# Diagonal blocks of a chunked triangular solve: 32x32 blocks inverted on VectorE, replaced by two 16x16 blocks per operation and a merge on TensorE

## The chip, the cores and the metric

The kernel runs on one NeuronCore of a Trainium2 chip. Its time is the device time of one execution in microseconds (us); the time of before is the median of three runs. Lower is better.

## The reference, cut to what matters

One layer of a hybrid backbone: a context of 256 tokens and 512 latent tokens pass through one input projection, then half of the channels through gated DeltaNet (8 heads of 128) and half through RWKV-7 (16 heads of 64), each in both directions, then through one output projection. Both mixers are computed in chunks of 64 tokens, and each chunk needs the inverse of a unit triangular 64x64 matrix. The DeltaNet one is written out in the reference:

```
lmat = jnp.where(strict, jnp.einsum('bhncd,bhnsd->bhncs', kb, k) * decay, 0.0)
eye = jnp.eye(CHUNK, dtype=jnp.float32)
tmat = lax.linalg.triangular_solve(eye + lmat, jnp.broadcast_to(eye, lmat.shape),
                                   left_side=True, lower=True, unit_diagonal=True)
u = tmat @ (v * beta[..., None])
wk = tmat @ (kb * jnp.exp(g)[..., None])
...
def step(state, inp):
    u_i, wk_i, attn_i, q_i, k_i, gl_i = inp
    v_new = u_i - wk_i @ state
    o_i = q_i @ state + attn_i @ v_new
    state = state * jnp.exp(gl_i)[..., None, None] + jnp.einsum('bhcd,bhce->bhde', k_i, v_new)
    return state, o_i
```

RWKV-7 is a scan over tokens in the reference; the kernel brings it to the same chunked form, so that one unit of work has three triangular systems (one DeltaNet head, two RWKV heads) for each chunk and direction.

## The kernel before, in words

The work is cut into 16 units, called mixers here and numbered 0 to 15: 0 to 7 are the eight head groups on the context (4 chunks each), 8 to 15 the same groups on the latents (8 chunks each). A mixer records these stages, each a method of class `Mix`:

- `prep_g`, `prep_r`, `prep_d`, `blocks` make, with TensorE transposes and products and DVE and ACT operations, the tile `Z` that holds all triangular matrices of the mixer. The transposes and products write PSUM tiles of the ring `pm` (two buffers, `br` in the rows), scratch goes to SBUF tiles of the ring `t` (four or five buffers).
- `send` writes the 32x32 diagonal blocks of `Z` to DRAM (`DA`), eight DMAs.
- `solve` reads them back with one block per partition (48 or 96 partitions, tile `solNL`), inverts them on DVE by 30 steps of elimination, two operations each (`solT`, then `solNL`), and writes them to DRAM (`DD`).
- `levels` loads them back and joins two 32x32 inverses into one of 64x64 by two bundles of 32x32 products on TensorE (`wm<-lt,Z`, then `pss<-Z,lt`).
- `chain` is the recurrence, 4 or 8 serial steps of small products, evacuations and state updates; one step on the latents begins with the ACT operation `Xs<-pss`.
- `outp` (latents only) norms, transposes and gates the result.

Around the mixers run the input projections (products of 128x128x512 or 128x128x256 on split fp32r halves: `hhi`, `hlo`, `chi`, `clo`, and `yh`, `yl` for the last four of 16 input tiles), the gate columns, and from latent group 3 (mixer 11) on the output projection, in four passes, whose products have `yh`, `yl` too. Latent groups 0 to 2 (mixers 8 to 10) use one lane of buffers, one after the other; from mixer 11 on two lanes alternate.

Nothing is ordered by hand. Class `Rec` records every operation and `Rec.schedule` plans the order of each engine when the program is built, by the operations' place in the recording, their dependencies and free buffers. Three rules of it matter here. When TensorE has nothing ready and has done little lately, the planner puts in a filler product on zeros (`wm<-zero`); projections marked as fills may be put anywhere that TensorE is free. A bundle is issued as a whole. And the buffers of a ring are given out in the order in which the recording created the tiles, not in the order in which they are ready:

```
                    e = t.pool.tags[t.key]
                    fs = [s for s in e[1] if s.free is not None]
                    if e[3] != t.order or not fs:
                        parked.setdefault((t.pool, t.key), []).append(o)
                        return
```

A mixer's stages are recorded whole before the next mixer's. All operations go through helpers, so every row of the profile has one line number, L705, and is told apart by its tiles.

Of the kernel before, what the change touches and what calls it, by code (L numbers as in the profile page):

```python
# [15 lines left out]
P = 128  # L16
DM = 2048
KT = DM // P
SEQ = 512
# [8 lines left out]

CST = {}
_off = 0  # L30
for _n, _w in (("ident", 128), ("bd", 128), ("mk0", 64), ("mk1", 64), ("sold", 4),
               ("mz0", 192), ("mz1", 192), ("scan", 512), ("ones", 128), ("cum0", 128), ("cum1", 128), ("hp0", 128), ("hp1", 128),
               ("sel", 2)):
    CST[_n] = (_off, _w)
    _off += _w
NCST = _off
NCST_KEEP, NCST_M = CST["mz0"][0], CST["ones"][0]
# [12 lines left out]
def constants():  # L50
    c = np.zeros((P, NCST), np.float32)

    def put(n, a):
        o, w = CST[n]
        c[:, o:o + w] = a

    i = np.arange(P)
    r, col = i[:, None], i[None, :]
    same = (r // 64) == (col // 64)
    s, t = r % 64, np.arange(64)[None, :]  # L60
    put("ident", np.eye(P))
    put("bd", same)
    put("mz0", np.concatenate([t > s, t >= s, t > s], 1))
    put("mz1", np.concatenate([t < s, t <= s, t < s], 1))
    put("mk0", np.where(t >= s, 0.0, -1e4))
    put("mk1", np.where(t <= s, 0.0, -1e4))
    put("scan", (np.arange(512)[None, :] % 64 != 0))
    put("ones", 1.0)
    row = np.arange(P)
    for ph, nj in ((0, 2), (1, 4)):  # L70
        d = (row // (3 * nj)) % 2
        c[:, CST["sold"][0] + 2 * ph] = -1.0 * (d == 0)
        c[:, CST["sold"][0] + 2 * ph + 1] = -1.0 * (d == 1)
    put("cum0", same & (r <= col))
# [11 lines left out]
def layout(inp):  # L86
# [22 lines left out]
    def put(n, a):  # L109
# [610 lines left out]
def bc(ap, shape):  # L720
    return ap.to_broadcast(list(shape))


class Mix:
# [250 lines left out]

    def send(self):
        k, i, ph, nj, S = self.k, self.i, self.ph, self.nj, self.k.S
        DA, DD = self.DD = [k.dp.tile([w, 4, 2, 3 * nj, 32, 32], F32, tag=f"{t}{ph}", bufs=2, name=k.nm(t))
                            for t, w in (("DA", 1), ("DD", 2))]
        DA = DA[0]  # L980
        for b in range(4):
            for d in range(2):
                S.dma_start(DA[b, d].rearrange("u s t -> s u t"), self.zdiag(b, d))

    def solve(self):
        k, i, ph, nb = self.k, self.i, self.ph, self.nb
        V, G, S = k.V, k.G, k.S
        (DA, DD), DA = self.DD, self.DD[0][0]
        N, L, tmp = k.solNL[:, 0], k.solNL[:, 1], k.solT
        m0 = k.cs("sold")[0:nb, 2 * ph:2 * ph + 1]  # L990
        m1 = k.cs("sold")[0:nb, 2 * ph + 1:2 * ph + 2]
        S.dma_start(L[0:nb], DA.rearrange("b d u s t -> (b d u) s t"))
        V.tensor_scalar_mul(N[0:nb], L[0:nb], m1)
        k.stt(N[0:nb], L[0:nb].rearrange("p s t -> p t s"), m0, N[0:nb], ALU.mult, ALU.add)
        G.memset(N[0:nb].rearrange("p s t -> p (s t)")[:, 0:1024:33], 1.0)
        for s in range(1, 31):
            r = 31 - s
            tv = tmp[0:nb, 0:r * s].rearrange("p (a b) -> p a b", b=s)
            shp = [nb, r, s]
            k.tt(tv, bc(N[0:nb, s + 1:32, s:s + 1], shp), bc(N[0:nb, s:s + 1, 0:s], shp), ALU.mult)  # L1000
            k.tt(N[0:nb, s + 1:32, 0:s], N[0:nb, s + 1:32, 0:s], tv, ALU.add)
        V.tensor_copy(L[0:nb], N[0:nb].rearrange("p s t -> p t s"))
        S.dma_start(DD.rearrange("w b d u s t -> (b d u) w s t"), k.solNL[0:nb])

    def levels(self):
        k, i, ph, nj, Z = self.k, self.i, self.ph, self.nj, self.Z
        V, S = k.V, k.S
        DN, DL = self.DD[1][0], self.DD[1][1]
        RT = self.t2("lt")[:, 0:96 * nj].rearrange("p (u t) -> p u t", t=32)
        for b in range(4):  # L1010
            bb = b % 2
            S.dma_start(RT[32 * b:32 * b + 32], (DN, DL)[bb][b, bb].rearrange("u s t -> s u t"))
            for d in range(2):
                S.dma_start(self.zdiag(b, d), (DL, DN)[d][b, d].rearrange("u s t -> s u t"))
        FC = (slice(32, 64), slice(0, 32))
        px = k.pmt("lx", "g")[:, 0:96 * nj].rearrange("p (u t) -> p u t", t=32)
        with k.rec.bundle():
            for j in range(nj):
                for e in range(3):
                    for b in range(4):  # L1020
                        d, q = b % 2, b // 2
                        rr, oo = slice(32 * b, 32 * b + 32), slice(32 * (b ^ 1), 32 * (b ^ 1) + 32)
                        k.mm(px[oo, e * nj + j], Z[rr, d, 2 * q + e, j, self.acol(q, FC[d])], RT[rr, e * nj + j])
        xs = self.t2("lt")[:, 0:96 * nj].rearrange("p (u t) -> p u t", t=32)
# [216 lines left out]
class Kernel:  # L1241
# [118 lines left out]
    def front(self):  # L1360
        S, V, A, G = self.S, self.V, self.A, self.G
# [10 lines left out]
        fc = {n: fp.tile([P, CST[n][1]], F32, name="f" + n) for n in ("ones", "sel")}  # L1372
# [47 lines left out]
        for kt in range(KT):  # L1420
            self.rec.shift = -self.cfg.get("fsh", 200)
            ps = self.pmt("ada", "g")[:, 0:256]
            for jj in range(2):
                j = 2 * kt + jj
                w = wa.pop(j)
                with self.rec.bundle():
                    for k in range(8):
                        g = k % 4
# [13 lines left out]
            t = fp.tile([P, 768], F32, tag="tmp", bufs=2, name=self.nm("ht"))  # L1442
# [12 lines left out]
            for k in range(4):  # L1455
                m = 128 if k == 3 else 96
# [9 lines left out]
        fp.release()  # L1466
        fq.release()
        lp = self.lp = self.pool("lp")
        self.solNL = lp.tile([96, 2, 32, 32], F32, name="solNL")
        self.solT = lp.tile([96, 256], F32, name="solT")  # L1470
# [9 lines left out]
        V.tensor_copy(self.cstm, fc[:, 0:NCST_M - NCST_KEEP])  # L1480

        def fcs(n):
            o, w = CST[n]
            return fc[:, o - NCST_KEEP:o - NCST_KEEP + w]

        e = self.cfg.get("eshift", 150)
        for k in range(4):
            mu, om = self.pc("mul", k)[0:96], self.dvo["oml"][0:96, k:k + 1]
            for ph in (1, 0):
# [3 lines left out]
                n, o = (512, 64) if ph else (256, 1)  # L1493
# [245 lines left out]

    def main(self):  # L1740
        self.u = {}
        self.tbufs = {"t": (4, 5), "lt": (1, 1), "ot": (0, 2), "dg": (1, 1)}
        self.mp = self.pool("mpA")
        defer = self.cfg.get("defer", [])
        for i in range(NSLOT):
# [199 lines left out]
```

## Time and profile before

| | |
|---|---|
| three runs | 2064.42, 2066.45, 2070.24 us; median 2066.45 us |
| profiled execution | 2065.16 us, of which the profile's span is 2063.4 us |
| TensorE (PE) busy | 1932.1 us, 94% |
| VectorE (DVE) busy | 1451.6 us, 70% |
| ScalarE (ACT), GpSimd (POOL) busy | 811.6 us, 575.9 us |
| mean granted TensorE clock | 0.977 |

A busy share is the time in which at least one instruction of the engine was under way. Matmuls overlap, and filler products count as busy, so that TensorE's real work is what is left after taking the fillers off. An fp32 product appears as two matmul records in the trace (pieces, below); one fp32r product is one.

### The profile page before, as it was taken

To read this page: it belongs to the slowest core of one execution; us is meant where nothing else is said; L and a number is where in the kernel's file an instruction comes from. 1 tells how busy PE (TensorE), PEld (TensorE's weight loads), DVE (VectorE), ACT (ScalarE), POOL (GpSimd) and SP (SyncE) were. 2 spreads that over 40 slices of the span, in tenths; PEclk is the share of its full clock that TensorE was granted. 3 is DMA by queue.
4 is the path that set the end of the run, shared out by engine and by line. 5 is a ranking of instruction groups with operands and counts; after the bars stand their busy time and mean duration, and the time that the engine had idled before them with its cause. 6 is when DMAs were issued, how large, how long until landed. Compare 5 with 4: busy or idle time off the path is not lost.

```text
span 2063.4 us, 43525 instructions
## 1 busy us (share of the span) xinstructions
PE 1932.1 (94%) x16575; PEld 1501.0 (73%) x16576; DVE 1451.6 (70%) x3397; ACT 811.6 (39%) x2127; POOL 575.9 (28%) x751
## 2 busy tenths in 40 slices
PE   7999999999999999999999999979778898889997
PEld 5678887877878787777777777767656666666666
DVE  5437587787877678684775784676678877778557
ACT  4443324333232433333443343444435362534335
POOL 0004314223150512100211211245234443343235
PEclk8999999999999999999999999999899999999998
DMA  8964343434333432344543454456232545143732
GB/s 313 362 215 132 107 118 97 111 85 109 91 102 94 106 111 66 99 112 133 159 137 86 120 144 112 125 171 205 74 82 56 164 143 153 52 110 105 257 107 93
DMA packets 230514, 269.28 MB, mean 131 GB/s; under 512 B 117280, under 2 KB 130080, under 8 KB 226208
## 3 DMA queue, kind: packets, MB, share of 16 engines
q1 hardware_dynamic: 230304, 266.49, 43.9%
q8 instruction: 130, 2.13, 0.4%
q14 instruction: 80, 0.66, 0.1%
HBM read 210.50 MB, written 55.89 MB: 129 GB/s over the span
## 4 chain that ended last, share of the span: by engine, by line
PE 68%; DVE 17%; DMA 6%; issue 3%; ACT 3%; POOL 2%; SPq 1%; DVEq 0%; ACTq 0%; POOLq 0%
PE accl L705 37%; PE accc L705 9%; PE br L705 8%; PE wm L705 7%; PE pss L705 7%; DVE solNL L705 3%; DVE Gk L705 2%; DVE solT L705 2%; DVE t L705 1%; SPq L705 1%; POOL gw L705 1%; DVE Z L705 1%; DMA solNL<-DA 1%; DMA gw<-wada 1%; DVE wl L705 1%
## 5 line engine op out<-in xcount | busy, mean ns | idle before, releaser
L705 ACT ACTIVATE wh<-wr 128x512 fp32r<-128x512 f32 x312 | 196.3, 629 | 398.5 <-PE accl L705 180.6
L705 PE MATMUL accl<-hhi,wl 128*128 128x512 f32 x768 | 314.2, 409 | 4.7 <-DVE wl L705 4.7
L705 PE MATMUL accl<-hhi,wh 128*128 128x512 f32 x768 | 310.9, 405 | 1.8 <-issue 1.8
L705 PE MATMUL accl<-hlo,wh 128*128 128x512 f32 x768 | 307.9, 401 | 0.0
L705 DVE TENSOR_TENSOR wl<-wr,wh 128x512 fp32r<-128x512 f32 x264 | 189.6, 720 | 105.7 <-ACT wh L705 99.5
L705 PE MATMUL accl<-yh,wh 128*128 128x512 f32 x480 | 207.8, 435 | 11.0 <-DVE Rr L705 5.4
L705 PE MATMUL accl<-yh,wl 128*128 128x512 f32 x480 | 199.6, 416 | 0.0
L705 PE MATMUL accl<-yl,wh 128*128 128x512 f32 x480 | 197.2, 411 | 0.4 <-POOL yl L705 0.4
L705 DVE TENSOR_TENSOR solNL<-solNL,solT 48x30 f32<-48x30 f32 (+29 forms) x480 | 171.4, 357 | 10.6
L705 PEld LDWEIGHTS accl<-hhi,wl 128*128 128x128 f32 x768 | 144.5, 188 | 41.7 <-DVE wl L705 6.6
L705 POOL TENSOR_TENSOR SRd<-Sbd,Dd 64x128 f32<-64x128 f32 x160 | 67.2, 420 | 379.1 <-DVE Sbd L705 372.9
L705 DVE TENSOR_TENSOR solT<-solNL 48x30 f32<-48x30 f32 (+29 forms) x480 | 165.8, 346 | 10.0
L705 PEld LDWEIGHTS accl<-hhi,wh 128*128 128x128 f32 x768 | 144.4, 188 | 20.9 <-issue 4.8
L705 PEld LDWEIGHTS accl<-hlo,wh 128*128 128x128 f32 x768 | 144.6, 188 | 19.7 <-issue 3.3
L705 PE MATMUL accc<-clo,wh 128*128 128x256 f32 x512 | 147.8, 289 | 0.0
L705 PE MATMUL accc<-chi,wh 128*128 128x256 f32 x512 | 146.2, 286 | 0.0
L705 PE MATMUL accc<-chi,wl 128*128 128x256 f32 x512 | 146.1, 285 | 0.0
L705 PE MATMUL wm<-zero 128*128 128x128 bf16 x1326 | 105.8, 232 | 22.8 <-DVE SG L705 7.7
L705 PEld LDWEIGHTS <-zero 128*128 128x128 bf16 x1344 | 91.2, 105 | 40.7 <-issue 36.1
L705 PEld LDWEIGHTS accl<-yh,wh 128*128 128x128 f32 x480 | 91.2, 191 | 36.6 <-issue 11.3
L705 PEld LDWEIGHTS accc<-clo,wh 128*128 128x128 f32 x512 | 96.4, 188 | 23.3 <-issue 0.5
L705 PEld LDWEIGHTS accc<-chi,wh 128*128 128x128 f32 x512 | 96.5, 189 | 20.8 <-issue 0.3
(320 smaller groups left out, 4139.2 us busy)
## 6 DMA issues: line engine op xcount, KB each, us to landing
wr<-win SPq DMA_DIRECT2D x256, 256.0 KB, 3.2
wa<-wada SPq DMA_DIRECT2D x32, 1024.0 KB, 6.3
gw<-wada SPq DMA_DIRECT2D x64, 256.0 KB, 3.5
ud<-Gk SPq DMA_DIRECT2D x64, 256.0 KB, 2.9
wr<-wout SPq DMA_DIRECT2D x64, 256.0 KB, 3.6
Rk<-ud SPq DMA_DIRECT2D x48, 256.0 KB, 3.0
rtd<-xt SPq DMA_DIRECT2D x48, 256.0 KB, 3.1
Rr<-rtd SPq DMA_DIRECT2D x48, 256.0 KB, 3.1
```

The lines of the kernel that those rows point to most:

```text
L705: r = getattr(self.engs[o.eng], o.fn)(*args, **kw)
```

## The change

The 32x32 elimination becomes one on 16x16 blocks: the two 16x16 diagonal blocks of a 32x32 block are eliminated by the same operation (`quads`), in 14 steps of two DVE operations in place of 30, and the off-diagonal 16x16 corner goes round the elimination (one ACT copy, one GpSimd memset). The layout in DRAM is changed with it. `levels` first joins two 16x16 inverses into one of 32x32: a bundle of products `px`, two operations that copy it to SBUF (`x0` on ACT, `x1` into the new tile `solX` on DVE), a second bundle of products (`pw`, `pt`), and copies back into `Z` and `RT` on both engines. For a context mixer these are 48 + 72 products, for a latent one 96 + 144, all with 16 moving columns, so 2 880 products or 5 760 pieces over the 16 mixers. `x0` is a tile of the ring `t` and `pt` one of the ring `pm`, which `levels` did not use before. The ring `u` of loaded projections has four buffers in place of five.

```diff
     def solve(self):
...
-        for s in range(1, 31):
-            r = 31 - s
-            tv = tmp[0:nb, 0:r * s].rearrange("p (a b) -> p a b", b=s)
-            shp = [nb, r, s]
-            k.tt(tv, bc(N[0:nb, s + 1:32, s:s + 1], shp), bc(N[0:nb, s:s + 1, 0:s], shp), ALU.mult)
-            k.tt(N[0:nb, s + 1:32, 0:s], N[0:nb, s + 1:32, 0:s], tv, ALU.add)
-        V.tensor_copy(L[0:nb], N[0:nb].rearrange("p s t -> p t s"))
-        S.dma_start(DD.rearrange("w b d u s t -> (b d u) w s t"), k.solNL[0:nb])
+        V.tensor_scalar_mul(N, L, m1)
+        for h in range(2):
+            k.stt(N[:, h], L[:, h].rearrange("p s t -> p t s"), m0, N[:, h], ALU.mult, ALU.add)
+        G.memset(X[:, 0:1024:33], 1.0)
+        k.act(corner(0), corner(1024), AF.Copy, scale=m1)
+        G.memset(corner(1024), 0.0)
+        for s in range(1, 15):
+            r = 15 - s
+            shp = [nb, 2, r, s]
+            tv = k.solT[0:nb, 0:2 * r * s].rearrange("p (h a b) -> p h a b", h=2, b=s)
+            k.tt(tv, bc(N[:, :, s + 1:16, s:s + 1], shp), bc(N[:, :, s:s + 1, 0:s], shp), ALU.mult)
+            k.tt(N[:, :, s + 1:16, 0:s], N[:, :, s + 1:16, 0:s], tv, ALU.add)
+        V.tensor_copy(L, N.rearrange("p h s t -> p h t s"))
...
     def levels(self):
...
+        with k.rec.bundle():
+            for d in range(2):
+                for u in range(nu):
+                    for b in range(4):
+                        k.mm(px[R32[b], d, u], dg(b, d, u), RT[R32[b], d, u, H[d]])
+        x0 = self.t2()[:, 0:16 * nu].rearrange("p (u t) -> p u t", t=16)
+        x1 = k.solX
+        m = k.cs("x16")
+        k.act(x0, px[:, 0], AF.Copy, scale=m[:, 0:1])
+        V.tensor_scalar_mul(x1[:, 0:nu, 16:32], px[:, 1], m[:, 1:2])
+        pw = k.pmt("lw", "r")[:, 0:32 * nu].rearrange("p (d u t) -> p d u t", d=2, t=16)
+        pt = k.pmt("lv")[:, 0:16 * nu].rearrange("p (u t) -> p u t", t=16)
+        with k.rec.bundle():
+            for u in range(nu):
+                for b in range(4):
+                    k.mm(pw[R16[b], 0, u], x0[R32[b], u], dg(b, 0, u, H[1]))
+            for u in range(nu):
+                for b in range(4):
+                    k.mm(pw[R32[b], 1, u], x1[R32[b], u], dg(b, 1, u, H[0]))
+            for u in range(nu):
+                for b in range(4):
+                    if b % 2:
+                        k.mm(pt[R16[b], u], dg(b, 1, u, H[0]), x1[R32[b], u, H[1]])
+                    else:
+                        k.mm(pt[R32[b], u], dg(b, 0, u), x0[R32[b], u])
+        for b in range(4):
+            k.act(dgs(R16[b], b, 0, H[1]), pw[R16[b], 0], AF.Copy)
+            V.tensor_copy(dgs(R32[b], b, 1, H[0]), pw[R32[b], 1])
+            if b % 2:
+                k.act(RT[R16[b], 1, :, H[1]], pt[R16[b]], AF.Copy)
+            else:
+                k.tt(RT[R32[b], 0, :, H[0]], RT[R32[b], 0, :, H[0]], pt[R32[b]], ALU.add)
...
-        t = self.u[(kind, i, 1)] = self.mp.tile([P, SEQ], F32, tag=tag, bufs=(5, 1)[tag == "uz"], name=self.nm(kind))
+        t = self.u[(kind, i, 1)] = self.mp.tile([P, SEQ], F32, tag=tag, bufs=(4, 1)[tag == "uz"], name=self.nm(kind))
```

Where the planner puts things is seen in the order of the built programs. The first place is TensorE at `levels` of mixer 12. Before, products of the stage `blocks` of mixer 13 (`br<-KR,BK`) stand on both sides of mixer 12's 32x32 products:

```order
L705 MATMUL br_0_134<-KR_2_12508,BK_5_9333 128x128
L705 MATMUL wm_0_129<-lt_0_9336,Z_0_9361 32x32 x48
L705 MATMUL br_1_135<-KR_1_12507,BK_7_9335 128x128
...
L705 MATMUL pss_0_130<-Z_0_9361,lt_0_9336 32x32 x48
L705 MATMUL br_1_135<-cst_60,Rk_4_9315 128x128 x4
```

Now mixer 13's first transposes (`br<-cst,t`) come only behind the last products of mixer 12's new merge (`br<-solX,Z`), and its `blocks` products stand within the steps of mixer 12's chain (`pss<-Xs,Z` is one step):

```order
L707 MATMUL br_1_135<-t_1_10068,Z_0_10109 32x16
L707 MATMUL br_1_135<-solX_1429,Z_0_10109 16x16
L707 MATMUL br_0_134<-cst_60,t_0_10067 128x128 x2
...
L707 MATMUL wm_0_129<-lt_0_10084,Z_0_10109 32x32 x48
...
L707 MATMUL pss_0_130<-Z_0_10109,lt_0_10084 32x32 x48
...
L707 MATMUL wm_0_129<-SG_0_10086,KQ_0_10110 128x128 x2
...
L707 MATMUL br_1_135<-KR_1_14387,BK_7_10083 128x128
L707 MATMUL br_0_134<-KR_1_14387,BK_7_10083 128x128
...
L707 MATMUL pss_0_130<-Xs_0_10090,Z_0_10109 64x64 x4
```

So a mixer's preparation moved from before the preceding mixer's `levels` to behind it. The second place is DVE during the solve of mixer 13. Before, its 63 operations are mixed with 93 others, most of them of mixer 12's chain (`SG`, `Sbd`, `VO`):

```order
L705 TENSOR_TENSOR solT_1428<-solNL_1427 96x198
L705 TENSOR_TENSOR t_1_9320<-br_1_135,ks_0_9324 128x512
L705 TENSOR_TENSOR Sbd_1429<-SRd_0_9340,pss_0_130 64x2x64 x2
L705 TENSOR_TENSOR SG_0_9338<-SGs_0_9341,wm_0_129 128x128
L705 TENSOR_TENSOR SG_0_9338<-SGs_0_9341,pss_0_130 128x128
L705 TENSOR_TENSOR solNL_1427<-solNL_1427,solT_1428 96x22x9
L705 TENSOR_TENSOR solT_1428<-solNL_1427 96x210
```

Now 32 operations stand among 19 others, which are of mixer 12's `outp` (`ot`, `omu`) and of the preparation of later stages (`bonus`, `dg`); the last 16 stand alone, and the merge follows:

```order
L707 SCALAR_TENSOR_TENSOR ot_0_10097<-bonus_0_10105,dv_66,Gz_0_10064 128x512
L707 TENSOR_TENSOR solNL_1427<-solNL_1427,solT_1428 96x2x9x6
L707 TENSOR_TENSOR solT_1428<-solNL_1427 96x112
L707 TENSOR_TENSOR solNL_1427<-solNL_1427,solT_1428 96x2x8x7
...
L707 COPY solNL_1427<-solNL_1427 96x2x16x16
L707 TENSOR_SCALAR solX_1429<-wm_0_129,cst_60 128x12x16
L707 TENSOR_TENSOR lt_0_10084<-lt_0_10084,br_0_134 32x12x16
L707 COPY Z_0_14382<-pss_0_130 32x12x16
```

The solve of each mixer from 12 on now begins where the preceding chain ends, not within it.

## Rows read from the trace of the kernel before

**Rows 1.** The page: its first line.

```profile
span 2063.4 us, 43525 instructions
```

**Rows 2.** Busy time by stretch: stretch, length, engines' busy us (instructions), clock, DMA.

```profile
265.00:1252.70 987.70, 972.67 (x7229) 775.02 (x7230) 725.04 (x1727) 366.63 (x949) 224.24 (x283) 1.00 0.40 110
1252.70:1531.60 278.90, 243.93 (x2391) 186.99 (x2390) 192.19 (x442) 117.12 (x319) 93.20 (x123) 0.95 0.43 124
1531.60:2063.40 531.80, 465.53 (x5046) 345.04 (x5045) 393.91 (x926) 228.47 (x653) 210.12 (x279) 0.96 0.43 125
```

**Rows 3.** The same stretches, instructions on zeros alone (fillers): PE, PEld, POOL.

```profile
265.00:1252.70 987.70, 1.16 (x3) 0.31 (x4) 0.00 (x0) 1.00 0.40 110
1252.70:1531.60 278.90, 33.64 (x393) 26.23 (x393) 0.00 (x0) 0.95 0.43 124
1531.60:2063.40 531.80, 55.51 (x670) 45.15 (x669) 0.00 (x0) 0.96 0.43 125
```

**Rows 4.** The same stretches, the tile solNL alone: sum over the span.

```profile
sum 2063.40, DVE 401.29 POOL 2.52; mean DVE 100.32 POOL 0.63
```

**Rows 5.** Timeline of DVE in solve of mixer 0: start, us, instruction.

```profile
274.86 0.74 DVE L705 TENSOR_SCALAR solNL<-solNL,cst 48x1024 f32<-48x1024 f32 x1
275.64 2.14 DVE L705 SCALAR_TENSOR_TENSOR solNL<-solNL,cst 48x1024 f32<-48x1024 f32 x1
277.81 0.20 DVE L705 TENSOR_TENSOR solT<-solNL 48x30 f32<-48x30 f32 x1
...
290.04 0.40 DVE L705 TENSOR_TENSOR solT<-solNL 48x240 f32<-48x240 f32 x1
```

**Rows 6.** Timeline of PE around bundles of 96 and of 48 pieces.

```profile
1091.42 0.40 PE L705 MATMUL accl<-yh,wl 128*128 128x512 f32 x1
1091.66 0.39 PE L705 MATMUL accl<-yh,wh 128*128 128x512 f32 x1
1091.98 1.02 PE L705 MATMUL wm<-lt,Z 32*32 32x32 f32 x96
1092.93 0.50 PE L705 MATMUL accl<-yl,wh 128*128 128x512 f32 x1
...
319.50 0.40 PE L705 MATMUL accl<-yl,wh 128*128 128x512 f32 x1
319.83 0.62 PE L705 MATMUL pss<-Z,lt 32*32 32x32 f32 x48
320.38 0.50 PE L705 MATMUL accl<-yh,wl 128*128 128x512 f32 x1
```

**Rows 7.** Timelines of DVE and PE: solve of mixer 13, its first 32x32 products.

```profile
1662.38 1.77 DVE L705 TENSOR_SCALAR solNL<-solNL,cst 96x1024 f32<-96x1024 f32 x1 [0.43 <-DMA solNL<-DA]
...
1734.60 1.03 DVE L705 COPY solNL<-solNL 96x1024 f32<-96x1024 f32 x1
...
1748.67 0.26 PE L705 MATMUL wm<-lt,Z 32*32 32x32 f32 x6
```

**Rows 8.** Busy time in chains 12 to 15 and the changeovers ahead of them.

```profile
1590.00:1657.00 67.00, 57.12 (x610) 41.83 (x607) 54.11 (x99) 26.05 (x72) 29.68 (x34) 1.00 0.58 163
1657.00:1711.00 54.00, 52.94 (x499) 37.58 (x500) 42.43 (x117) 30.40 (x96) 24.29 (x37) 1.00 0.43 120
1711.00:1760.00 49.00, 39.71 (x508) 30.18 (x506) 36.13 (x76) 12.27 (x32) 15.97 (x17) 0.86 0.54 146
1811.00:1863.00 52.00, 44.68 (x522) 33.77 (x522) 40.63 (x80) 15.24 (x39) 22.16 (x23) 0.93 0.51 142
1916.00:1941.00 25.00, 24.20 (x315) 16.76 (x312) 12.86 (x24) 9.46 (x25) 8.90 (x9) 1.00 0.78 227
1941.00:1994.00 53.00, 49.32 (x450) 34.11 (x450) 26.22 (x80) 17.23 (x47) 7.47 (x18) 0.94 0.50 167
```

**Rows 9.** Groups of instructions by shape: count, busy us, mean ns, idle before.

```profile
L705 DVE COPY SV<-pss 64x128 f32<-64x128 f32 x96 | 27.5, 287 | 38.2 <-PE pss L705 35.6 <-ACT junk L705 1.0 <-ACT t L705 0.6
L705 DVE TENSOR_SCALAR Z<-pss 32x384 f32<-32x384 f32 x16 | 9.0, 560 | 12.7 <-ACT Z L705 6.9 <-PE br L705 3.3 <-PE accl L705 2.4
```

More of the change, by code (lines that the diff above doesn't have):

```diff
@@ L30 @@
 _off = 0
-for _n, _w in (("ident", 128), ("bd", 128), ("mk0", 64), ("mk1", 64), ("sold", 4),
+for _n, _w in (("ident", 128), ("bd", 128), ("mk0", 64), ("mk1", 64), ("sold", 4), ("x16", 2),
                ("mz0", 192), ("mz1", 192), ("scan", 512), ("ones", 128), ("cum0", 128), ("cum1", 128), ("hp0", 128), ("hp1", 128),
-               ("sel", 2)):
+               ("sel", 2), ("e16", 16)):
     CST[_n] = (_off, _w)
@@ L70, in constants @@
     for ph, nj in ((0, 2), (1, 4)):
-        d = (row // (3 * nj)) % 2
+        d = (row // (12 * nj)) % 2
         c[:, CST["sold"][0] + 2 * ph] = -1.0 * (d == 0)
         c[:, CST["sold"][0] + 2 * ph + 1] = -1.0 * (d == 1)
+    put("x16", np.concatenate([-1.0 * (r % 32 >= 16), 1.0 * (r % 32 < 16)], 1))
+    put("e16", (r % 32 == np.arange(16)[None, :]))
     put("cum0", same & (r <= col))
@@ L977, in send @@
         k, i, ph, nj, S = self.k, self.i, self.ph, self.nj, self.k.S
-        DA, DD = self.DD = [k.dp.tile([w, 4, 2, 3 * nj, 32, 32], F32, tag=f"{t}{ph}", bufs=2, name=k.nm(t))
+        DA, DD = self.DD = [k.dp.tile([w, 2, 3 * nj, 4, 32, 32], F32, tag=f"{t}{ph}", bufs=2, name=k.nm(t))
                             for t, w in (("DA", 1), ("DD", 2))]
-        DA = DA[0]
         for b in range(4):
             for d in range(2):
-                S.dma_start(DA[b, d].rearrange("u s t -> s u t"), self.zdiag(b, d))
+                S.dma_start(DA[0, d, :, b].rearrange("u s t -> s u t"), self.zdiag(b, d))
     def solve(self):
@@ L987, in solve @@
         V, G, S = k.V, k.G, k.S
-        (DA, DD), DA = self.DD, self.DD[0][0]
-        N, L, tmp = k.solNL[:, 0], k.solNL[:, 1], k.solT
+        (DA, DD), X = self.DD, k.solNL[0:nb]
         m0 = k.cs("sold")[0:nb, 2 * ph:2 * ph + 1]
         m1 = k.cs("sold")[0:nb, 2 * ph + 1:2 * ph + 2]
-        S.dma_start(L[0:nb], DA.rearrange("b d u s t -> (b d u) s t"))
-        V.tensor_scalar_mul(N[0:nb], L[0:nb], m1)
-        k.stt(N[0:nb], L[0:nb].rearrange("p s t -> p t s"), m0, N[0:nb], ALU.mult, ALU.add)
@@ L995, in solve, with quads @@
[L995 to L1003 removed]
+        def quads(o):
+            x = X[:, o:o + 1056].rearrange("p (h y) -> p h y", y=528)[:, :, 0:512]
+            return x.rearrange("p h (s t) -> p h s t", t=32)[:, :, 0:16, 0:16]
@@ new lines, in corner @@
+        def corner(o):
+            return X[:, o:o + 1024].rearrange("p (s t) -> p s t", t=32)[:, 16:32, 0:16]
+        N, L = quads(0), quads(1024)
+        S.dma_start(X[:, 1024:2048], DA[0].rearrange("d u b s t -> (d u b) (s t)"))
+        V.tensor_scalar_mul(N, L, m1)
[4 more added lines that the diff above has]
+        G.memset(corner(1024), 0.0)
@@ new lines, in solve @@
+        for s in range(1, 15):
[5 more added lines that the diff above has]
+        V.tensor_copy(L, N.rearrange("p h s t -> p h t s"))
+        S.dma_start(DD.rearrange("w d u b s t -> (d u b) w (s t)"), X[:, 0:2048].rearrange("p (w x) -> p w x", w=2))
@@ L1005, in levels @@
     def levels(self):
         k, i, ph, nj, Z = self.k, self.i, self.ph, self.nj, self.Z
-        V, S = k.V, k.S
-        DN, DL = self.DD[1][0], self.DD[1][1]
-        RT = self.t2("lt")[:, 0:96 * nj].rearrange("p (u t) -> p u t", t=32)
+        V, S, nu = k.V, k.S, 3 * self.nj
+        DD = self.DD[1]
+        RT = self.tl([P, 64 * nu], "lt").rearrange("p (d u t) -> p d u t", d=2, t=32)
+        for d in range(2):
+            S.dma_start(RT[:, d], DD[d, d].rearrange("u b s t -> (b s) u t"))
@@ L1010, in levels @@
         for b in range(4):
-            bb = b % 2
-            S.dma_start(RT[32 * b:32 * b + 32], (DN, DL)[bb][b, bb].rearrange("u s t -> s u t"))
             for d in range(2):
-                S.dma_start(self.zdiag(b, d), (DL, DN)[d][b, d].rearrange("u s t -> s u t"))
+                S.dma_start(self.zdiag(b, d), DD[1 - d, d, :, b].rearrange("u s t -> s u t"))
+        R32 = [slice(32 * b, 32 * b + 32) for b in range(4)]
+        R16 = [slice(32 * b, 32 * b + 16) for b in range(4)]
+        H = (slice(0, 16), slice(16, 32))
@@ new lines, in levels, with dg, dgs @@
+        px = k.pmt("lx", "g")[:, 0:32 * nu].rearrange("p (d u t) -> p d u t", d=2, t=16)
+        def dg(b, d, u, c=slice(0, 32)):
+            e, j = divmod(u, nj)
+            o = 32 * (b % 2)
+            return Z[R32[b], d, 2 * (b // 2) + e, j, self.acol(b // 2, slice(o + c.start, o + c.stop))]
+        def dgs(rr, b, d, c):
+            q, o = b // 2, 32 * (b % 2)
+            return Z[rr, d, 2 * q:2 * q + 3, :, self.acol(q, slice(o + c.start, o + c.stop))].rearrange("p e j m -> p (e j) m")
@@ new lines, in levels @@
+        with k.rec.bundle():
+            for d in range(2):
+                for u in range(nu):
[7 more added lines that the diff above has]
+        pw = k.pmt("lw", "r")[:, 0:32 * nu].rearrange("p (d u t) -> p d u t", d=2, t=16)
@@ L1468, in front @@
         lp = self.lp = self.pool("lp")
-        self.solNL = lp.tile([96, 2, 32, 32], F32, name="solNL")
-        self.solT = lp.tile([96, 256], F32, name="solT")
+        self.solNL = lp.tile([96, 2080], F32, name="solNL")
+        G.memset(self.solNL, 0.0)
+        self.solT = lp.tile([96, 112], F32, name="solT")
+        self.solX = lp.tile([P, 12, 32], F32, name="solX")
         self.Sbd = lp.tile([P, 2, 2, P], F32, name="Sbd")
@@ L1480, in front @@
         V.tensor_copy(self.cstm, fc[:, 0:NCST_M - NCST_KEEP])
+        o = CST["e16"][0] - NCST_KEEP
+        V.tensor_copy(self.solX[:, :, 0:16], bc(fc[:, o:o + 16].unsqueeze(1), [P, 12, 16]))
         def fcs(n):
@@ L1741, in main @@
         self.u = {}
-        self.tbufs = {"t": (4, 5), "lt": (1, 1), "ot": (0, 2), "dg": (1, 1)}
+        self.tbufs = {"t": (4, 5), "ot": (0, 2), "dg": (1, 1)}
         self.mp = self.pool("mpA")
```

4 lines of the change are left out of this document (2 added, 2 removed).

## The prediction

> **What bounds the kernel now.** I read busy time by stretch first, because the page's averages mix stages with different limits. From 265 to 1252.7 us TensorE is busy 972.7 of 987.7 us, and only 1.2 us of that are fillers [rows 2, 3]: here the kernel is bound by TensorE's work, and whatever DVE saves can win no more than the 15.0 us in which TensorE stood still. From 1252.7 to 1531.6 us (the end of mixer 10's turn and the first products of mixer 11) TensorE stands still for 35.0 us and spends 33.6 us on fillers; from 1531.6 to the end it stands still for 66.3 us, with 55.5 us of fillers [rows 2, 3]. In these two stretches the kernel waits for the serial path of a mixer: preparation, solve, levels, chain.
>
> The last stretch has a rhythm that the reader can see in the changeovers [rows 8]: a chain takes 53 to 54 us whether DVE is busy for 42.4 us in it or for 26.2, and between one chain and the next lie 67, 49, 52 and 25 us. In mixer 13's changeover the solve began at 1662.4, inside chain 12, and was done at 1735.6, 25 us after the chain had ended; its first 32x32 products came at 1748.7, 13 us later [rows 7]. The solve needs 25.1 us of DVE per mixer (401.3 us over 16) [rows 4], but is spread over 73 us here, because DVE does the chain, the output stage and the next preparation in between.
>
> **The change, part by part.** *DVE.* In the old elimination an operation on 30 elements takes 0.20 us and one on 240 takes 0.40 us [rows 5], so about 0.17 us plus 0.95 ns per element. The new one has 28 operations with 2 240 elements in all: 4.8 + 2.1 = 6.9 us. The operations around it (0.74, 2.14 and 1.03 us [rows 5, 7]) keep half of their elements: 2.0 us. So a solve goes from 25.1 to about 9 us. The merge gives back seven operations of at most 192 elements; by copies from PSUM of 128 elements (0.29 us) and of 384 (0.56 us) [rows 9] that is 0.36 us each, 2.5 us. Net 13.6 us less DVE for each mixer. In the stretch that TensorE bounds this is worth nothing by itself.
>
> *TensorE.* A product of 512 columns holds TensorE for 0.24 us. With 96 pieces between two of them 1.27 us pass, with 48 pieces 0.88 us [rows 6]; so the bundles take 1.03 and 0.64 us, which is 0.25 us per bundle and 8.1 ns per piece. The new pieces have 16 moving columns, which the trace does not show. At the price of 32 columns the new bundles (96 and 144 pieces for a context mixer, 192 and 288 for a latent one) cost 2.45 and 4.39 us, 55 us in all; with half the price per piece 1.47 and 2.45 us, 31 us in all. A price of nothing or a gain is excluded, since nothing on TensorE is removed. I take 47 us (2.1 and 3.75 us per mixer), nearer the upper end, because most of the weights loaded are still 32x32 and only the moving side is halved.
>
> On this price a rule of the Trainium skill speaks against the change. The row gives 8.1 ns per piece [rows 6]. The page "TensorE: Matmul & The Clock Gate" (section "Wait — 56ns, not 53.3ns?") says that matmuls start no closer than about 25 ns however few columns they have; by it the 5 760 pieces would be 144 us. The trace does not bear it out where four groups of 32 rows take turns; it comes back as the last rival.
>
> *Where the mixers stand.* The ring `t` and the ring `pm` now hold a tile of `levels`, and rings are given out in the order of recording; so the order of the changed program has mixer 13's preparation behind mixer 12's merge, inside chain 12, where before it ran beside solve 12. The solve then starts where a chain ends. What is late next is the chain itself. I add up a changeover: solve 9 us and the 19 other operations in it about 9, together 18; back through DRAM 13 [rows 7]; the two new bundles and their copies 7; from the first 32x32 products to the chain's first step 10 (1748.7 to about 1760 in mixer 13, [rows 7, 8]). That is 48 us, against 67, 49, 52 and 25 now, a sum of 192 against 193. So in the tail the faster solve is spent on the overlap that is lost.
>
> *Stretch by stretch.* By its order, the new program needs 32 fillers and not 389 up to mixer 11's products, since mixers 8 to 10 get through sooner and the projections last until then: 357 fillers at 0.086 us (33.6 us for 393) are 31 us less. The waits there should fall from 35.0 to about 7 us: the stretch ahead has 15.0 in 987.7 us, which makes 4, and 32 fillers bring a few more; 28 us less. Bounds: no change, and all of the 35. Behind mixer 11's products the order has 829 fillers where 661 stood: 168 at 0.083 us are 14 us more. How TensorE's waits there move follows from the length: changeovers as before, and chains 12 to 14 and 11 longer by about 5 us each, since they now hold all of the preparation's products and, in chain 12, 84 output products of 0.24 us, on an engine that was busy 52.9 of 54 us in that chain already [rows 8]. That is 532 - 1 + 20 = 551 us. TensorE's work is 465.5 now, plus 15 for four merges, 7 for 31 output products that move here from the stretch ahead (they count there as 7 less), plus 14 of fillers: 502. So the waits are 49 us, 17 less.
>
> *At nothing:* the DMAs of `levels` go from 12 to 10 on SP's queue; the one-time setup of `solNL` and `solX` lies in the stretch that TensorE bounds. Four buffers of `u`: a mixer's fifth and sixth load wait for the first two to be used up, but are read only in the late stages, beside `send` and the solve's way through DRAM. If that cover is gone, a changeover has a landing more.
>
> **Sum.** +47 (products) - 31 - 28 (fillers and waits up to mixer 11) + 14 - 17 (the same behind it) = -15 us. The span goes from 2063.4 [rows 1] to 2048 us, the profiled execution's 2065.2 to 2050, and since the median of the three runs stands 1.3 us above that execution, a median of 2051 us. About 0.3% (6 us) is what a measurement of this kernel can tell from no change.
>
> **The rivals.** *The solve hides after all.* In the order, the last products of `blocks` of mixer 13 stand three steps before the end of chain 12. If `send` and part of the solve fit in there, a changeover is 38 us: four times 10 less, 2011 us. For it: a chain takes 53 us at little DVE load as at much. Against: the order of DVE has `outp` inside the solve.
>
> *The overlap lost costs more than the solve gives: slower.* DVE works in order, so a solve operation behind one of `outp` that waits for GpSimd or for TensorE's transposes waits too. DVE is busy 40.6 of 52 us in the changeover ahead of chain 14 even now [rows 8]. If the solve takes 28 us and not 18, changeovers are 58 us, four of them 40 us more: 2091 us. It decides from a changeover of 52 us on (15 us over four). For it also: the order has more fillers behind mixer 11 than before, which the planner puts in only where TensorE has nothing to do.
>
> *A wash.* Pieces at their full price (55, not 47) and waits up to mixer 11 that fall by 18 and not 28: 2069 us, no change. For it: in the stretch that TensorE bounds every added product is paid in full.
>
> *The floor of 25 ns.* If pieces of 16 columns started 25 ns apart, the products would cost 144 us and not 47, most of it where TensorE is the bound: 2148 us. Against it are the bundles of the same shape of tiles.
>
> **Chances.** Forecast (2036 to 2060) 0.45, hidden solve 0.16, wash 0.16, lost overlap 0.19, floor 0.04. Nearly all of the first (0.43) and the second are faster by over 0.3%: 0.59; the rest of the first and the wash are within: 0.18; slower 0.23. The range of 2018 to 2086 holds the forecast and the wash, and of the rivals on either side the part in which a changeover is off by less than 9 us.
>
> **What would show it.** DVE busy about 1 230 us, a solve of 9 us of DVE; bundles of 192 pieces in 1.3 to 1.8 us; mixer 11's first 32x32 products near 1497 us (1531.6 - 31 - 28 - 7, and 32 of the 47 us), with TensorE busy throughout up to there; changeovers near 48 us with the solve at their start. The prediction is wrong if bundles cost far more than 8 ns per piece, if TensorE waits in the turns of mixers 8 to 10, or if changeovers are under 40 or over 55 us.

## The result, and the profile after

The changed kernel takes 2151.2 us (median of four runs, 2144.3 to 2156.1), before took 2068.3 us beside it: a ratio of 1.040, interval 1.0361 to 1.0438. It is 4% slower, and 65 us above the range of the prediction. The profiled execution took 2156.1 us with a span of 2154.3 us.

The page of after, its first rows and the row of one of its instruction queues:

```profile
span 2154.3 us, 54495 instructions
...
PE 1998.9 (93%) x22147; PEld 1556.4 (72%) x22147; DVE 1258.3 (58%) x3014; ACT 852.4 (40%) x2255; POOL 564.2 (26%) x768
...
q8 instruction: 173, 2.83, 0.6%
```

DVE did what was said (1258 us, predicted 1230). Queue q8 had 130 packets before; 173 packets of 2.83 MB are 16 KB each, and 2 x 22147 weight loads and products over 173 packets are 256: it is TensorE's instruction stream, 256 instructions to a packet.

Busy time by stretch, cut as [rows 2] at the first 32x32 products of mixers 9 and 11, and under it fillers alone (as [rows 3]) and the sum for solNL (as [rows 4]):

```profile
265.00:1247.50 982.50, 953.71 (x9870) 764.78 (x9869) 590.22 (x1458) 370.74 (x989) 222.40 (x294) 0.98 0.37 105
1247.50:1541.40 293.90, 274.67 (x3177) 209.53 (x3177) 180.71 (x410) 132.82 (x350) 84.91 (x118) 0.95 0.47 135
1541.40:2154.30 612.90, 520.06 (x7213) 388.58 (x7212) 350.05 (x846) 249.44 (x712) 208.97 (x292) 0.92 0.39 114
...
1247.50:1541.40 293.90, 3.92 (x36) 2.38 (x36) 0.00 (x0) 0.95 0.47 135
1541.40:2154.30 612.90, 67.23 (x837) 55.19 (x837) 0.00 (x0) 0.92 0.39 114
...
sum 1889.30, DVE 156.61 ACT 8.07 POOL 7.45; mean DVE 52.20 ACT 2.69 POOL 2.48
```

Mixer 11's products come at 1541.4, not 1497 us. The fillers up to there went as the order said, but TensorE still stands still for 28.8 + 19.2 = 48.0 us up to there (before 50.0; the prediction had 22), and its tail is 612.9 us long, not 551.

What TensorE waited for, in us, times and the longest; "issue" is a wait for nothing that the profile shows. These four rows are all that after has of it on TensorE, 62.0 us in 35 waits; before had 6.8 us in 5:

```profile
PE pss L707 <- issue: 22.9, 14, 3.5
PE br L707 <- issue: 19.2, 12, 2.5
...
PE accl L707 <- issue: 10.1, 4, 4.3
...
PE wm L707 <- issue: 9.8, 5, 3.9
```

25 of the 35 (46.8 us) stand inside the new bundles, four more in the 32x32 products that follow. Timeline of PE in mixer 8's, and in mixer 3's first:

```profile
1070.54 1.39 PE L707 MATMUL wm<-lt,Z 32*32 32x16 f32 x139
1074.17 0.63 PE L707 MATMUL wm<-lt,Z 32*32 32x16 f32 x53 [2.24 <-issue]
...
1076.30 0.70 PE L707 MATMUL pss<-Z,t 32*16 32x16 f32 x67
1078.46 0.35 PE L707 MATMUL pss<-Z,t 32*16 32x16 f32 x27 [1.46 <-issue]
...
579.52 1.04 PE L707 MATMUL wm<-lt,Z 32*32 32x16 f32 x96
```

A bundle of 192 pieces that all read the same two tiles stops after 139, for 2.24 us, and goes on. The 96 pieces run through. The same row stood in the trace of before, where I passed over it; its timeline of PE ahead of chain 12:

```profile
1649.20 0.72 PE L705 MATMUL pss<-Z,lt 32*32 32x32 f32 x61
1652.35 0.50 PE L705 MATMUL pss<-Z,lt 32*32 32x32 f32 x35 [2.43 <-issue]
```

The changeovers ahead of chains 12 to 15 of after (as [rows 8]), and chain 12:

```profile
1603.10:1674.00 70.90, 53.67 (x963) 38.83 (x962) 29.15 (x67) 27.23 (x77) 20.39 (x24) 0.88 0.49 133
1674.00:1730.10 56.10, 56.10 (x548) 39.84 (x549) 40.98 (x105) 29.83 (x91) 28.66 (x45) 1.00 0.46 131
1730.10:1793.70 63.60, 53.99 (x1041) 42.44 (x1039) 31.05 (x67) 24.13 (x74) 16.63 (x20) 0.84 0.43 131
...
1848.50:1913.90 65.40, 49.56 (x984) 37.43 (x985) 28.11 (x69) 24.96 (x76) 17.37 (x19) 0.87 0.42 110
...
1966.60:2041.60 75.00, 63.64 (x966) 45.78 (x962) 32.05 (x72) 19.35 (x46) 9.14 (x11) 0.84 0.63 199
```

They are 71, 64, 65 and 75 us where 48 was forecast. Solve 12 begins at 1610.5, behind chain 11, and ends at 1632.2; the merge begins at 1645.1, the 32x32 products at 1665.7.

### The profile page after: what moved, and what is told of

Same layout as the page of the kernel before. It is cut to its first block, busy times and chain, and to the rows that moved or that the text cites. A ratio compares the mean times of both kernels' runs of the same rounds, so it can differ in the third digit from the quotient of the medians.

```text
span 2154.3 us, 54495 instructions
## 1 busy us (share of the span) xinstructions
PE 1998.9 (93%) x22147; PEld 1556.4 (72%) x22147; DVE 1258.3 (58%) x3014; ACT 852.4 (40%) x2255; POOL 564.2 (26%) x768
## 3 DMA queue, kind: packets, MB, share of 16 engines
q8 instruction: 173, 2.83, 0.6%
## 5 line engine op out<-in xcount | busy, mean ns | idle before, releaser
L707 PE MATMUL accl<-hlo,wh 128*128 128x512 f32 x768 | 313.2, 408 | 0.0
L707 PE MATMUL accl<-yl,wh 128*128 128x512 f32 x480 | 201.9, 421 | 0.4 <-POOL yl L707 0.2
L707 PEld LDWEIGHTS accl<-yl,wh 128*128 128x128 f32 x480 | 93.8, 196 | 23.8 <-issue 9.6
L707 PEld LDWEIGHTS accl<-yh,wl 128*128 128x128 f32 x480 | 93.5, 195 | 23.2 <-issue 4.3
L707 PE MATMUL wm<-zero 128*128 128x128 bf16 x1137 | 87.0, 231 | 17.8 <-ACT vn L707 8.2
L707 DVE SCALAR_TENSOR_TENSOR Gk<-accl,par,Gk 128x510 f32<-128x510 f32 (+5 forms) x113 | 82.8, 733 | 25.3 <-ACT Gk L707 24.7
```

The lines of the kernel that those rows point to most:

```text
L707: r = getattr(self.engs[o.eng], o.fn)(*args, **kw)
```

## The experiments

Two theories. **A:** TensorE's instructions run out in the bundles. **B:** overlap is lost, because two tiles of the merge stand in the rings that the next preparation uses. A wait for data inside the merge, and a cost of 25 ns for each start, are the rivals of A.

**burst**, TensorE alone, and **burst_dma**, the same beside loads:

```diff
+            mm(t[r, 16 * c:16 * c + 16], src[r, 32 * c:32 * c + 32], src[r, 256 + 16 * c:272 + 16 * c], start=True, stop=True)
...
+    wide(120)
+    for n in (48, 96, 144, 192, 288, 384, 576):
+        pieces(two, n)
+        wide(60)
...
+    for n in (96, 192, 384):
+        full(full_, n)
+        wide(60)
```

> A kernel of nothing but TensorE work, its output all zeros: bursts of small products with 60 products of 512 columns between two of them (120 ahead of the first). First bursts of 48, 96, 144, 192, 288, 384 and 576 pieces of the merge's shape (32x16, four groups of 32 rows in turn, two pieces for each fp32 product); then 384 pieces cut into eight groups of 48 with 2, 4 and 8 wide products behind each; then 192 and 384 one-pass bf16 pieces; then 96, 192 and 384 products of 128x128 weights by 16 columns. No burst waits for data. Theory A (the instructions run out): a piece is two instructions, and the profile of the changed kernel shows TensorE's instruction queue bring 256 instructions in a packet, in the long bundles one per 3.6 to 4.1 us, so one piece per 28 to 32 ns once what is at hand is used up. By it bursts of 48 and 96 run at about 8 ns per piece, and longer ones show single stalls of 1 to 2.5 us between pieces of 8 ns: 288 pieces take 5 to 7 us and 576 pieces 12 to 16 us; the groups cut by 8 wide products show no stall (2.1 us per group), those cut by 2 do. Theory B (a wait for data, a buffer or a copy in the mixer): nothing of the kind is here, so every burst takes 8 to 9 ns per piece, 576 pieces about 5 us. Theory C (each start costs about 25 ns, whatever came before): 48 pieces take 1.2 us already, and all bursts lie on one line of 25 ns per piece with no single stall.

> The burst kernel again, with 64 loads of 1 MB from DRAM running beside it on SP's queue and read by nobody; TensorE's instructions and their order are the same. In the quiet run a stall lasted 2.0 to 2.7 us and came after each 128 pieces, while in the changed kernel single stalls last from 0.3 to 4.5 us, and in one of the experiments 8.4 us, beside loads of 256 KB each. If the instructions come through the same DMA engines as the data and queue behind it, the stalls here grow, to 3 to 8 us while loads run, and the same bursts (192 pieces and more) have them. If they have a way of their own, the stalls stay at 2.0 to 2.7 us and the long ones in the kernels have another cause.

Timeline of PE of burst (144, 192 and 288 pieces, then 384 products of full tiles by 16 columns):

```profile
56.63 1.39 PE L34 MATMUL two<-w 32*32 32x16 f32 x144
...
71.01 1.41 PE L34 MATMUL two<-w 32*32 32x16 f32 x147
73.42 0.56 PE L34 MATMUL two<-w 32*32 32x16 f32 x45 [1.01 <-issue]
...
86.97 1.44 PE L34 MATMUL two<-w 32*32 32x16 f32 x151
90.69 1.90 PE L34 MATMUL two<-w 32*32 32x16 f32 x128 [2.27 <-issue]
94.69 0.31 PE L34 MATMUL two<-w 32*32 32x16 f32 x9 [2.10 <-issue]
...
316.75 10.01 PE L39 MATMUL full<-z 128*128 128x16 bf16 x384
```

and of burst_dma, the 288 pieces:

```profile
91.99 1.44 PE L34 MATMUL two<-w 32*32 32x16 f32 x151
98.16 1.90 PE L34 MATMUL two<-w 32*32 32x16 f32 x128 [4.73 <-issue]
104.36 0.30 PE L34 MATMUL two<-w 32*32 32x16 f32 x9 [4.29 <-issue]
```

A comes out but for one size (288 pieces took 8.0 us, not 5 to 7). 48, 96 and 144 pieces run without a wait in 0.59, 0.99 and 1.39 us, 8.3 ns for each further piece. In the longer bursts TensorE first stops after 147 to 255 pieces, by where the burst began, and from there on after each 128 pieces, which are 256 instructions, one packet of the queue. With nothing to wait for, 128 pieces take 4.00 us from restart to restart here (94.69 - 90.69) and 3.5 to 4.0 us over all bursts, 27 to 31 ns per piece. Groups of 48 with two wide products between them still stopped twice, with four or eight never. In all 12 such waits of burst the products go on 1.2 to 1.5 us after the end of a packet of that queue in the trace; in after 33 of the 35 do. Beside loads that keep the DMA engines busy (share 0.93 to 0.99) the same 128 take 6.20 us; behind the last load, at about 180 us, the waits are those of the quiet run again (2.2 and 2.6 us in the 384 one-pass pieces, 2.0 and 2.6 there). So instructions come more slowly beside data, as they would if they queued with it; where they meet is not shown. No fixed price per start does this: full tiles by 16 columns need 26 ns each (10.01 us for 384), with no stop. 26 ns is close to the pace at which the instructions come, and a longer run of full tiles was not tried.

The clock comes on top. 60 wide products stand behind each burst, 58 of them recorded; busy time behind 192 and behind 288 pieces:

```profile
74.15:86.97 12.82, 12.77 (x58) 5.68 (x58) 0.00 (x0) 0.00 (x0) 1.00 0.01 1
95.33:110.77 15.44, 15.38 (x58) 6.37 (x59) 0.00 (x0) 0.00 (x0) 0.83 0.00 1
```

The granted clock fell to its lower level, 1.2 GHz, at 90.4 us, at the end of the first stop in the 288 pieces, and was back at 100.6 us; the same wide products cost 2.6 us more. It fell in the run of 384 full tiles too, at 322.5 us, where nothing had stopped, so the stops are not shown to be its only cause.

**no_merge** and **half_units**, all or half of the merge left out:

```diff
-        px = k.pmt("lx", "g")[:, 0:32 * nu].rearrange("p (d u t) -> p d u t", d=2, t=16)
...
-                k.tt(RT[R32[b], 0, :, H[0]], RT[R32[b], 0, :, H[0]], pt[R32[b]], ALU.add)
```

```diff
+        nh = nu // 2
...
-                for u in range(nu):
+                for u in range(nh):
```

> The changed kernel without the merge: the two bundles of 32x16 products, the copies behind them and the tiles x0, x1, pw and pt are left out, so the corners of the 32x32 inverses stay zero and the output is not the reference's. The 16-row solve, its DMAs and the four buffers stay. Theory A (instructions run out in the bundles): the time falls by the 47 us of products that the sum had, by about 68 us of stalls inside the bundles that the trace shows as gaps over 0.3 us, less what of it lies in TensorE's waits anyway, and by the latency of the merge in four changeovers: about 2020 to 2050 us. Theory B (the loss is overlap, since the preparation comes behind the levels in the rings t and pm): the preparation now stands free again, so this too is faster, but the bundles themselves are worth no more than 47 us plus 7 us in each of five changeovers: 2060 to 2080 us.

> The changed kernel with the merge for half of the units alone (three of six, or six of twelve): bundles of 48 and 72 pieces for a context mixer, 96 and 144 for a latent one, the copies behind them half as wide. The output is not the reference's, since the other half's corners stay zero. All waits, rings and steps of the merge stay. Theory A: stalls grow faster than the pieces once a bundle is longer than what is at hand, so halving wins more than half of what leaving out the merge wins where the bundles are long; gaps over 0.3 us inside bundles fall from 68 us to under 20 us, and the time to about 2060 to 2090 us. Theory B: the rings and the order of the steps are the same, so only half of the pieces' 47 us and of the copies is won: 2115 to 2130 us.

no_merge took 1926.2 us (0.931, 0.9276 to 0.9344), below what either theory gave: the faster solve alone wins 141 us, the merge takes 225 us. half_units took 2065.2 us (0.9992, 0.9967 to 1.0017), its waits for instructions 11.6 us: that lies in A's range, but halving won 86 of the 225 us, less than half, which A did not say: what the rings cost is paid with half a merge too, and the changeovers of half_units are still 63 to 71 us. Busy time of no_merge in the same three stretches, and the sum of its fillers there:

```profile
265.00:1168.70 903.70, 898.73 (x6950) 719.18 (x6949) 576.78 (x1387) 355.90 (x927) 230.09 (x296) 1.00 0.41 112
1168.70:1446.00 277.30, 265.36 (x2325) 201.25 (x2327) 190.07 (x416) 126.57 (x337) 83.53 (x117) 0.99 0.48 138
1446.00:1928.70 482.70, 448.33 (x4771) 328.52 (x4770) 336.96 (x799) 237.31 (x673) 216.33 (x290) 0.97 0.52 150
...
sum 1663.70, PE 36.56 PEld 28.38 POOL 0.00; mean PE 12.19 PEld 9.46 POOL 0.00
```

**own_rings** takes both tiles of the merge out of the rings `t` and `pm`; **own_x0** and **own_pt** take out one:

```diff
-        x0 = self.t2()[:, 0:16 * nu].rearrange("p (u t) -> p u t", t=16)
+        x0 = k.solNL[:, 1024:1024 + 16 * nu].rearrange("p (u t) -> p u t", t=16)
...
-        pt = k.pmt("lv")[:, 0:16 * nu].rearrange("p (u t) -> p u t", t=16)
+        pt = px.rearrange("p d u t -> p (d u) t")[:, 0:nu]
```

> The changed kernel with x0 in a part of solNL that is free at that time and the product pt in the bank of px, so that no tile of the merge stands in the rings t and pm, and the next mixer's preparation need not follow the merge. Theory A: the bundles are as long as before and stall as before, 68 us in gaps over 0.3 us; the time moves by less than 15 us. Theory B: the preparation is back beside the solve, changeovers fall from 64 to 83 us to about 50 us: 2080 to 2110 us.

> The changed kernel with x0 in a part of solNL, so that no tile of the merge stands in the ring t, while the product pt stays in the ring pm. With both out of their rings the time was 2073 us, with both in it 2151 us. If the ring t of the preparation's vectors is what puts the next preparation behind the merge, this run gives nearly all of the 78 us: 2070 to 2095 us, with solve 12 to 15 beginning inside the chain ahead. If it is the ring pm, through which every transpose and every product of the preparation passes, the time stays at 2135 to 2155 us and solve 12 to 15 begin where a chain ends.

> The changed kernel with the product pt in the bank of px, so out of the ring pm, while x0 stays in the ring t. Moving x0 alone gave 2145 us and moving both 2073 us. If the ring pm alone puts the next preparation behind the merge: 2065 to 2085 us, with solve 12 to 15 beginning inside the chain ahead. If either tile in its ring is enough to do so: 2135 to 2155 us.

own_rings took 2072.9 us (1.0021, 0.9998 to 1.0044): 78 us less than the change, just below B's range, and TensorE's waits for instructions are 60.2 us, much as in the change (62.0). own_x0 took 2145.4 us (1.0375, 1.033 to 1.042) and own_pt 2163.6 us (1.0461, 1.0418 to 1.0503), 9 us above its range: either tile is enough to hold the next preparation, as a ring gives out its tiles strictly in the order of recording. DVE's first operation of solve 12, in after, own_x0 and own_pt, where the last step of chain 11 begins at 1603.1, 1606.2 and 1606.0, so behind it:

```profile
1610.50 0.48 DVE L707 TENSOR_SCALAR solNL<-solNL,cst 96x512 f32<-96x512 f32 x1
...
1607.60 0.47 DVE L707 TENSOR_SCALAR solNL<-solNL,cst 96x512 f32<-96x512 f32 x1
...
1611.87 0.47 DVE L707 TENSOR_SCALAR solNL<-solNL,cst 96x512 f32<-96x512 f32 x1
```

and in own_rings, where chain 11 runs from 1567.5 to 1615.7:

```profile
1569.41 0.48 DVE L707 TENSOR_SCALAR solNL<-solNL,cst 96x512 f32<-96x512 f32 x1
```

Busy time of own_rings in the changeover ahead of chain 12, then in the three stretches, with the sum of its fillers there:

```profile
1615.70:1654.20 38.50, 29.83 (x877) 23.54 (x876) 22.83 (x45) 11.61 (x34) 10.45 (x14) 0.82 0.23 59
...
265.00:1241.80 976.80, 952.24 (x9885) 759.96 (x9885) 591.23 (x1459) 372.27 (x1000) 223.84 (x296) 0.98 0.38 106
1241.80:1559.60 317.80, 293.66 (x3279) 222.72 (x3278) 202.19 (x445) 142.50 (x374) 104.37 (x137) 0.94 0.49 140
1559.60:2074.60 515.00, 453.90 (x6629) 337.24 (x6628) 331.32 (x807) 236.72 (x675) 191.85 (x271) 0.94 0.44 126
...
sum 1809.60, PE 36.20 PEld 26.90 POOL 0.00; mean PE 12.07 PEld 8.97 POOL 0.00
```

The solve is back inside the chain, and the changeovers are 39, 49, 48 and 41 us. The 78 us are a balance: behind mixer 11's products own_rings is 98 us shorter than the change, up to them 18 us longer (1559.6 against 1541.4); there solve 11 is spread over 52 us and not 25.

**u4**, before with four buffers of `u`:

```diff
-        t = self.u[(kind, i, 1)] = self.mp.tile([P, SEQ], F32, tag=tag, bufs=(5, 1)[tag == "uz"], name=self.nm(kind))
+        t = self.u[(kind, i, 1)] = self.mp.tile([P, SEQ], F32, tag=tag, bufs=(4, 1)[tag == "uz"], name=self.nm(kind))
```

> The kernel before with four buffers of u instead of five and nothing else changed. The prediction costed this part at nothing. Theory A (instructions run out in the bundles) and theory B (overlap lost through the rings t and pm) both leave it there: 2062 to 2075 us. If the fifth buffer hid landings, the changeovers behind mixer 11 get longer by a landing each and the time goes above 2080 us.

2072.1 us (1.0027, 1.0004 to 1.0051): about 5 us, hardly told from nothing; in its profile 4.5 of the 7 us are there by mixer 0's first 32x32 products, before a latent buffer is loaded.

**spaced** is own_rings with bundles of at most 96 pieces and a planner that counts instructions; **own_cut** has the cut without the count, **cut_only** both, with the rings as the change has them:

```diff
+        def stock(t):
+            return min(cap, credit + (t - at) / per)
...
+            elif e == "T" and (fills or len(r) > 1) and r and r[0][1].bun and r[0][1].cls[0] == 32 and stock(s) < 2 * r[0][1].passes * len(r[0][1].bun.ops):
+                big = [x for x in r if x[1].cls[0] > 32]
+                r = [min(big)] if big else fills if fills else r
```

> own_rings with the merge's bundles cut into groups of at most 96 pieces, and the planner keeping count of TensorE's instructions: 256 at hand, one more each 13 ns (256 in 3.3 us, as the stalls of the burst kernel come out: 2.1 to 2.5 us after each 128 pieces that take 1.0 us); a group for which not enough are at hand is put behind wide products, where there are any ready. The same products are computed. Theory A (stalls come from the instructions): gaps over 0.3 us between pieces fall from 55 us to under 20 us, less time is spent at the half clock, and up to mixer 11 the kernel gains 20 to 40 us; behind it, where TensorE has no other work to put between, little. 2030 to 2060 us. If the stalls were waits of the merge itself (copies, landings) and not the instructions, cutting the bundles removes none of them, and each cut costs about 0.25 us more: 2073 to 2090 us.

> own_rings with the bundles cut into groups of at most 96 pieces as in spaced, but without the planner's count of instructions, so that groups follow each other as soon as they are ready. It tells whether spaced won its 45 us by the cut or by the count. If by putting wide products between the groups (theory A): stalls inside runs of pieces stay near the 49 us of own_rings, 2060 to 2080 us. If by the finer grain (waits of the first group only for its own operands, other work between): 2025 to 2045 us.

> The changed kernel with the merge's bundles cut into groups of at most 96 pieces and the planner's count of instructions, as in spaced, but with x0 and pt in the rings t and pm as the change has them. If the stalls of the instructions and the overlap lost through the ring are two separate costs, the cut wins here what it won beside own_rings, 45 us: 2095 to 2120 us. If they are one cost (the stalls matter only because the changeovers are bare), it wins less than 20 us up to mixer 11 and most behind it, or nothing: 2130 to 2150 us.

spaced took 2027.7 us (0.981, 0.9769 to 0.9851), 2 us below A's range, own_cut 2075.2 us (1.0041, 1.0019 to 1.0063): the count, which puts wide products between the groups, wins the 45 us, the cut by itself nothing. 28 us of them are waits for instructions; the mean granted clock is higher too, 0.973 against 0.966. TensorE's largest waits for instructions in own_cut (56.3 us in all) and in spaced (28.1 us):

```profile
PE wm L710 <- issue: 29.6, 15, 4.7
PE pss L710 <- issue: 20.8, 15, 2.7
```

```profile
PE wm L725 <- issue: 14.6, 10, 3.2
...
PE pss L725 <- issue: 9.4, 12, 1.9
```

28.1 us are more than the 20 us of gaps that A allowed. The count adds 256 instructions per 3.3 us, and burst shows 3.5 to 4.0; whether the rest of the waits comes from that was not tried.

cut_only took 2153.7 us (1.0419, 1.037 to 1.0467): no gain, 4 us above the range that takes both for one cost. Its waits for instructions fell to 44.4 us in all, but behind mixer 11 its changeovers are as bare as in the change (64 to 82 us). Ahead of it, mixer 11's products came 17 us later than in after; one wait of 8.2 us for instructions lies there, beside loads (DMA share 0.84 as it began, 0.54 behind that). What the rest is stays open.

**flip** is spaced without the product `pt`, DVE turning the blocks over instead:

```diff
-                k.mm(pt[R32[b], u], dg(b, 0, u), x0[R32[b], u])
...
+            V.transpose(RT[R32[b], b % 2], dgs(R32[b], b, b % 2, slice(0, 32)))
```

> spaced with the product pt left out of TensorE's work: the corners of RT come from the merged blocks in Z, turned over by DVE, 32x32 at a time, one operation for each 32 rows in place of the four copies from pt. The output stays the reference's. TensorE has 96 pieces less in a latent and 48 less in a context mixer, 1152 in all. By theory A they are worth between 8 ns (9 us) and the 26 ns at which the instructions come (30 us), less 0.5 us of DVE in each turn behind the copies: 2000 to 2020 us. If pieces cost no more than their own 8 ns, the DVE operations on the path eat that: 2022 to 2035 us.

2018.5 us (0.9759, 0.9722 to 0.9795), the fastest of all that compute the whole layer: 2.4% faster than before, 6% faster than the change. That is 9 us less than spaced for 1152 pieces less, but the intervals of the two overlap, and the waits for instructions did not fall (32.5 us against 28.1), so the price of 26 ns for such a piece is not borne out.

## Why the prediction was wrong

Two terms of it failed in size, both on the side of loss; a third, the gain, was too small as well.

**The price of the merge: 47 us for its products, measured 147 in all.** The step that failed was "0.25 us per bundle and 8.1 ns per piece", read from bundles of 48 and 96 pieces [rows 6] and carried on to 192 and 288. From no_merge to own_rings, where the rings do no harm, the merge costs 147 us. By the rows from 265 us on, the work it adds on TensorE is 88 us (1699.8 busy of 1809.6 us in own_rings, less 36.2 of fillers, against 1612.4 less 36.6), and TensorE stands still 58 us longer (109.8 against 51.3); its waits for instructions are 60.2 us there and 3.4 in no_merge. 114 of the 147 us come up to mixer 11's products (1559.6 against 1446.0), 32 behind them. The price holds up to a stock of instructions; behind it a piece costs 27 to 31 ns in burst, more beside loads. Of the 88 us of work the pieces themselves are 65 (8.1 ns each would be 47); the rest lies in the other products, with the clock at 0.94 in the last two stretches of own_rings against 0.99 and 0.97. The bound of 55 us came from the same short bundles, so the range could not hold this.

The rival with a floor of 25 ns gave 2148 us. That this is close to what was measured is luck, since its mechanism is not what the runs show: 96 pieces ran at 10 ns, full tiles at 26. The Trainium skill's rule (page "TensorE: Matmul & The Clock Gate", section "Wait — 56ns, not 53.3ns?") agrees with the full tiles alone. The page that bears on the cause is "Runtime: NRT & Kernel Launch", section "Instruction fetch mechanics": instructions come in blocks of 16 KiB (256 instructions), ahead of need. The packets agree in size. It also says that this is mostly hidden, since instructions issue more slowly than blocks arrive; here a piece takes 8 ns, while its two instructions arrive at 27 to 31 ns per piece, and for runs of such pieces the measurement decides against it.

**The changeovers: 48 us, measured 69 on average.** "The solve then starts where a chain ends" was right, and it was the rival of lost overlap that came, with a bigger price: the four changeovers were 83 us longer than forecast (275 against 192), where that rival had 40. Of the sum 18 + 13 + 7 + 10, over the four changeovers, the solve was done 26 us after the chain, the merge began 16 us later, the 32x32 products 19 us behind that, the chain 8 us later. The new bundles are the worst of it, 19 us instead of 7: theory A inside theory B. I had this loss in the order and priced it at about nothing against the old changeovers (192 against 193); what it had to be held against is 176 us, what they are in own_rings, with the fast solve, the merge and the overlap kept.

**The gain: 31 + 28 us, and 17 in the tail; measured 141 where nothing stands against it.** With the merge gone, and the overlap kept, TensorE's fillers and standstill from 265 us on fall from 90.3 + 116.3 [rows 2, 3] to 36.6 + 51.3 us, 119 us. The gain up to mixer 11 was there to be had, but the stalls took its place (48.0 us of standstill, not 22; 34.6 of them are waits for instructions).

**Right:** DVE's work (9.8 us per solve), the 32 fillers left up to mixer 11, four buffers at about nothing. Chains 11 to 14 were 2.5 us longer on average, not 5. The steps from before over no_merge and own_rings to the change are -141 for the solve, +147 for the merge and +78 for the rings. They add up to the 84 us by construction, and the prices hold in this order alone: with the tiles back in the rings, in cut_only, what won 45 us beside own_rings won nothing.

## What to carry to other kernels

A price per instruction from a short run of small products is not the price in a long one: where the engine uses up instructions faster than blocks of them land, look for waits that the profile puts down to nothing, and put wide work between. Before adding a step, list which rings it takes a tile from and what is recorded behind it. Price a gain and its obstacles by leaving the obstacle out first: the kernel without the merge showed at once that 141 us were on the table.

## What the runs showed of the hardware that was not expected

TensorE ran 147 to 255 small pieces in a row without a wait, by where the burst began, then no more than 128 per 3.5 to 4.0 us, or per 6.2 us while loads kept the DMA engines at 420 GB/s. Up to 384 products of full tiles, at 26 ns each, did not wait. Whether the instruction queue can be served ahead of the data was not tried.
